# A two-layer encoder trunk on one core: PSUM evacuation by ACT, a mean ahead of a weight split, and a later retention turn

## Chip, cores and metric

The kernel runs on one core of a Trainium2 chip. The metric is the device time of one execution in microseconds (us); smaller is better.

## The reference, cut to what matters

Two layers work on x of 256 positions by 1024 features. Each layer is a half-step SwiGLU FFN, a mixer, and another half-step FFN; every part begins with an RMSNorm whose scale, shift and gate come from a conditioning vector c.

```python
for l in range(DEPTH):                                        # DEPTH = 2
    cond = (silu(c) @ ada_w[l] + ada_b[l])                     # 9 vectors of 1024
    sh1, sc1, g1, sh2, sc2, g2, sh3, sc3, g3 = jnp.split(cond, 9)
    x = x + 0.5 * g1 * swiglu(modulate(rmsnorm(x, norm_g[l, 0]), sh1, sc1), ffn1_w13[l], ffn1_w2[l])
    x = x + g2 * hybrid_mixer(modulate(rmsnorm(x, norm_g[l, 1]), sh2, sc2), w_in[l], w_out[l], ...)
    x = x + 0.5 * g3 * swiglu(modulate(rmsnorm(x, norm_g[l, 2]), sh3, sc3), ffn2_w13[l], ffn2_w2[l])
return rmsnorm(x, final_g)
```

The mixer projects to four groups (forgetting attention "fox", mLSTM, retention "ret", state space "ssd"), each with four heads of 64, and joins them by w_out. The FFN's inner width is 2816.

## The kernel before

**Layout and precision.** The residual lives transposed in SBUF (xT: eight tiles k of 128 features by 256 positions). Every large product is made of three matmuls per 128-by-128 weight tile (mm3, lines 238 to 240): each operand is a rounded high part and a low remainder, and high x high, high x low and low x high are added. The weights arrive by DMA as raw tiles of 512 KB (four slots, NRAW, issued by SP), and `split` makes the parts: ACT copies raw to whi (line 220), DVE subtracts to wlo (line 221). `wload` is one DMA and one split per raw tile.

**Order.** The program is traced in Python, and a scheduler at compile time lays the instructions out per engine: by priority, which is program order, among those it takes to be ready at that time by its own estimates. On the chip each engine then runs its own list strictly in that order, with semaphores between engines. `tc.add_manual_dep(..., NoSync ...)` adds an edge to that layout alone; it makes no wait of its own. POOL (here: InOrder, line 105 in the profile) keeps the traced order.

**The statistics.** Each RMSNorm is started before its statistics are known: `pre_tile` makes the parts of xT times the scale (uh, ul), and the first projections run on those. In `mm_two` the first pair of projections runs six of the eight tiles k (KS), then `stat_end` puts in the sum of squares (line 367, PE), the mean on ACT (line 388, `stat_rs`), and the power -0.5 on POOL; then the pair goes on with its last two k. The next pair runs KR = 2 tiles k of its first half, and only then `st.rows()` spreads the factors over the partitions by matmuls (line 394) and ACT copies them to R (line 398). PE stands behind POOL's power there. `norm_h` then makes the normed h from R for all later projections. In the FFN the pairs are c = 0, 1, 2; in the mixer they are the projections rq, rk and sx.

**The mixer's steps.** ORDER names the steps one after another: p.x is the projection of x, the others work on its results. Steps with a `yield` are continued each time their name comes again. PSUM has four banks of tag a (projections), three of tag b (everything small in the mixer and R) and one of tag c (sums). `row_sums` turns the gate sums into rows: a bank b, two copies by ACT (lines 860 and 861) and one subtraction by DVE from PSUM (line 862), of eight partitions. `ret_front` then wants three banks b (lines 1131 and 1136). `put_y` is the way of each mixer's result y to the output projection: four transposes into a bank b (`to_fm`, line 817), a copy to yh by ACT (line 827) and a subtraction to yl by DVE from PSUM (line 828). Retention's result ry is made at step rg (line 1247) and turned there at once. The tag "cin" of the mixer's pool has one slot; `copied` uses it to take the convolutions' inputs out of PSUM (line 1147).

**Background loads.** The conditioning vectors of later parts are made beside the main work: `ada_load` is a DMA of 512 KB (araw) and a reduction on DVE (line 279). BG holds how many such loads follow each projection: pairs (m, n) mean n loads over the next m calls of `background`. In the mixer one araw slot is used (MB = 1).

Of the kernel before, what the change touches and what calls it, by code (L numbers as in the profile page):

```python
# [9 lines left out]
F32 = mybir.dt.float32  # L10
F32R = mybir.dt.float32r
AF = mybir.ActivationFunctionType
# [35 lines left out]
NRAW = 4  # L48
NSP = 3
KS = 6  # L50
KR = 2
BG = [((16, 17), (1, 0), (7, 14), (3, 4)), ((8, 0), (6, 13)), ((2, 0), (13, 18), (5, 0), (10, 14)), ((2, 0), (13, 18), (5, 0), (10, 14)),
      ((8, 0), (6, 8)), ((3, 0), (14, 8))]
R0 = 6
MB = 1
NW = 11, 0, 2, 6
# [1 line left out]
LF = 10  # L58

ORDER = """p.rq p.rk h clear p.sx p.mv rqe rke rq gates rk p.sbc mv sxe sx sbc p.rv rv p.mq rows ssd ret p.mk ssd mq ret  # L60
 p.sz ssd mk mlstm p.rg sz ssdb p.fk rg mlstm p.fq ssdb fk mlstm p.fv fq mlstm fox p.mo fv fox mo""".split()

WO_STEPS = {1: "fox", 3: "turn", 5: "turn"}
RAW = ("rq", "rk", "sx")
# [5 lines left out]
def trunk_kernel(  # L70
# [134 lines left out]


    spare = [None, 0]

    def split(raw):

        a, b = raw.shape[1:]
        v = lambda t: t[:, : a * b].rearrange("p (a b) -> p a b", a=a)
        pl, n = wp, NHW
        if spare[0] is not None:
            spare[1] = (spare[1] + 1) % (NHW + NSP)
            if spare[1] >= NHW:
                pl, n = spare[0], NSP
        hi = v(pl.tile([P, HW], F32R, tag="whi", name="whi", bufs=n))
        lo = v(pl.tile([P, HW], F32R, tag="wlo", name="wlo", bufs=n))
        act.activation(out=hi, in_=raw, func=AF.Copy)  # L220
        dve.tensor_tensor(out=lo, in0=raw, in1=hi.bitcast(F32), op=ALU.subtract)  # L221
        return hi, lo

    def raw_tile():
        return wp.tile([P, HW], F32, tag="raw", name="raw", bufs=NRAW)

    def wload(src, n, a, b):

        out = []
        for i in range(n):  # L230
            raw = raw_tile()[:, : a * b]
            sp.dma_start(out=raw, in_=src[:, i * a * b:(i + 1) * a * b])
            out.append(split(raw.rearrange("p (a b) -> p a b", a=a)))
        return out

    def mm3(o, w, x, first, last, **kw):
# [149 lines left out]
    def stat_rs(sums):  # L386
        v = tp.tile([P, 2], F32, tag="rs", name="rs")
        act.activation(out=v, in_=sums, func=AF.Identity, scale=1.0 / D, bias=epsc)
        pool.tensor_tensor(out=v, in0=v, in1=half[:, :2], op=ALU.pow)
        return v  # L390

# [146 lines left out]
    def ffn_in(fp, l, i, w13, w2, st, done):  # L538
# [20 lines left out]
        if first:  # L559
            h, os = st  # L560
            for c in range(NS):
                o = os[c].rearrange("p (a b) -> p a b", a=2)
                gate_out(c, o[:, 0, :], o[:, 1, :])
        else:
            def evac(c, og, oa):
                v = tp.tile([P, 4], F32, tag="fb", name="fb")
                act.activation(out=v[:, 0:1], in_=oa[:, T:T + 1], func=AF.Copy)
                act.activation(out=v[:, 2:3], in_=og[:, T:T + 1], func=AF.Copy, scale=0.5)
                g = fp.tile([P, T], F32, tag="gR", name="gR", bufs=2)
                a = fp.tile([P, T], F32, tag="aR", name="aR", bufs=2)  # L570
                dve.tensor_tensor(out=g, in0=og[:, :T], in1=st.R, op=ALU.mult)
                dve.tensor_tensor(out=a, in0=oa[:, :T], in1=st.R, op=ALU.mult)
                gate_out(c, a, g, v[:, 0:1], v[:, 2:3])

            pend = None
            for c in range(ND):
                w = wload(w13(l, c), 2, KT, P)
                og, oa = bank_a()[:, :TS], (bank_b() if c < 2 else bank_a())[:, :TS]
                mm_two((og, oa), w, (st.uh, st.ul), st)
                if c:  # L580
                    evac(*pend)
                if c == NN:
                    h = norm_h(st)
                pend = (c, og, oa)
            evac(*pend)
# [146 lines left out]
    def mixers_in(mp, l, st, done):  # L732
# [17 lines left out]

        def proj_first(name):

            w = wload(wfm[l, FM.index(name)], 2, KT, P)
            background()
            os = [bank_a()[:, :TS] for _ in range(2)]
            mm_two(os, w, (st.uh, st.ul), st)
            r = mp.tile([P, 2, TS], F32, tag=dict(rq="rawrq", rk="ml", sx="rl")[name], name="raw" + name)
            for j in range(2):
                act.activation(out=r[:, j, :], in_=os[j], func=AF.Copy)
            return r  # L760
# [63 lines left out]

        def put_y(m, o):
            h = yh[:, m].rearrange("p a b -> p (a b)")
            act.activation(out=h, in_=o, func=AF.Copy)
            dve.tensor_tensor(out=yl[:, m].rearrange("p a b -> p (a b)"), in0=o, in1=h.bitcast(F32), op=ALU.subtract)

        def pv_tm(pt0, pt1, v):  # L830

# [10 lines left out]
        def row_sums(g):  # L842
# [16 lines left out]
            pe.matmul(o[:, T:T + P], lhsT=gi[:, 1, :], rhs=ident, start=False, stop=True)  # L859
            act.activation(out=rows[:8], in_=o[:8, :3 * P], func=AF.Copy)  # L860
            act.activation(out=rt[32:40], in_=o[32:40, :3 * P], func=AF.Copy)
            dve.tensor_tensor(out=rows[32:40], in0=o[32:40, :3 * P], in1=rt[32:40].bitcast(F32), op=ALU.subtract)
            return rows

        def add_row(o, rows, r, first=True, last=False):
# [378 lines left out]
        def e_rg():  # L1244
            r2 = tm_silu2(v["org"], "g2", rw(R_RG, 256))
            y = mp.tile([P, 2, 256], F32, tag="y", name="ry", bufs=2)
            dve.scalar_tensor_tensor(out=y, in0=r2, scalar=0.5, in1=v["rl"].rearrange("p t h d -> p t (h d)"),
                                     op0=ALU.mult, op1=ALU.mult)
            put_y(2, to_fm(y))

        def e_h():
# [176 lines left out]
```

## Time and profile before

| | |
|---|---|
| three runs | 1073.56, 1071.71, 1073.25 us; median 1073.25 us |
| the profiled execution | 1072.46 us, of which the span from the first to the last instruction is 1070.7 us |
| granted TensorE clock | 0.998 of full speed |
| busy: PE / DVE / ACT / POOL | 1049.5 / 857.2 / 544.6 / 65.4 us |

The span is what the profile's rows are measured in; the time around it (1.76 us here) is not in them. Starts in the rows are microseconds from the start of the span. Layer 0's mixer runs from about 208 to 350 us, layer 1's from about 728 to 870 us, so a place in layer 1's mixer lies about 520 us behind its twin. A matmul's listed duration is modelled and overlaps the next one; what counts for PE is the distance from start to start.

### The profile page before, as it was taken

How to read it: one execution, taken by the hardware profiler on the slowest of the kernel's cores; microseconds unless marked ns; L12 is line 12 of the kernel's file. 1: busy time of each engine (PE TensorE's matmuls, PEld its weight loads, DVE VectorE, ACT ScalarE, POOL GpSimd, SP SyncE). 2: the span in 40 equal slices, each digit the busy share in tenths (PEclk: the TensorE clock that was granted, in tenths of full speed). 3: DMA queues.
4: the chain of work that ended last, by engine and by line, in shares of the span. 5: the costliest groups of instructions: out<-in, count | busy, mean ns of one | idle time of the engine just before them, and what ended most of it. 6: DMA issues, size and time to landing. Idle time of an engine off the chain costs nothing. (4 is left out here: it accounts for less than half of the span.)

```text
span 1070.7 us, 21683 instructions
## 1 busy us (share of the span) xinstructions
PE 1049.5 (98%) x8725; PEld 1035.1 (97%) x8725; DVE 857.2 (80%) x1503; ACT 544.6 (51%) x904; POOL 65.4 (6%) x87
## 2 busy tenths in 40 slices
PE   8999999999999999999999999999999999999997
PEld 6999999998999999999999999999999999999997
DVE  6899888699877998888688998767988689866551
ACT  4565544375446745533474543356636466454441
POOL 0000001110101100000100000011000020000010
PEclk9999999999999999999999999999999999999999
DMA  9899888854466689987568998766546366765541
GB/s 365 345 322 358 308 320 301 278 179 148 145 221 211 210 289 328 326 300 274 184 217 288 324 321 295 268 217 190 175 130 217 120 216 231 269 218 186 182 136 40
DMA packets 74023, 258.29 MB, mean 241 GB/s; under 512 B 10178, under 2 KB 12610, under 8 KB 73411
## 3 DMA queue, kind: packets, MB, share of 16 engines
q1 hardware_dynamic: 73634, 256.39, 69.7%
q8 instruction: 68, 1.11, 0.4%
q10 hardware_dynamic: 288, 0.52, 0.1%
q14 instruction: 33, 0.26, 0.1%
HBM read 255.83 MB, written 1.05 MB: 240 GB/s over the span
## 5 line engine op out<-in xcount | busy, mean ns | idle before, releaser
L220 ACT ACTIVATE whi<-raw 128x1024 fp32r<-128x1024 f32 (+1 forms) x340 | 353.5, 1046 | 276.1 <-PE pa L239 69.1
L221 DVE TENSOR_TENSOR wlo<-raw,whi 128x1024 fp32r<-128x1024 f32 (+1 forms) x340 | 409.0, 1209 | 90.3 <-ACT whi L220 89.3
L238 PE MATMUL pa<-hh,whi 128*128 128x256 f32 x1392 | 395.4, 284 | 0.8 <-ACT whi L220 0.8
L240 PE MATMUL pa<-hh,wlo 128*128 128x256 f32 x1392 | 393.1, 282 | 0.5 <-DVE wlo L221 0.5
L239 PE MATMUL pa<-hl,whi 128*128 128x256 f32 x1392 | 392.9, 282 | 0.0
L238 PEld LDWEIGHTS pa<-hh,whi 128*128 128x128 f32 x1392 | 267.0, 192 | 3.2 <-issue 1.8
L240 PEld LDWEIGHTS pa<-hh,wlo 128*128 128x128 f32 x1392 | 265.1, 190 | 0.7 <-DVE wlo L221 0.7
L239 PEld LDWEIGHTS pa<-hl,whi 128*128 128x128 f32 x1392 | 265.0, 190 | 0.6 <-issue 0.5
L279 DVE CUSTOM_DVE_ANT_0 araw<-araw,cact 128x1024 f32<-128x1024 f32 x128 | 156.5, 1224 | 46.8 <-DMA araw<-in_ada_dram 46.5
L238 PE MATMUL pa<-sh,whi 128*128 128x256 f32 x660 | 184.2, 279 | 0.0
L240 PE MATMUL pa<-sh,wlo 128*128 128x256 f32 x660 | 184.2, 279 | 0.0
L239 PE MATMUL pa<-sl,whi 128*128 128x256 f32 x660 | 184.2, 279 | 0.0
L238 PEld LDWEIGHTS pa<-sh,whi 128*128 128x128 f32 x660 | 125.1, 190 | 0.0
L240 PEld LDWEIGHTS pa<-sh,wlo 128*128 128x128 f32 x660 | 125.1, 190 | 0.0
L239 PEld LDWEIGHTS pa<-sl,whi 128*128 128x128 f32 x660 | 125.0, 189 | 0.0
L555 ACT ACTIVATE sh<-s 128x256 fp32r<-128x256 f32 x88 | 36.2, 412 | 102.5 <-DVE s L548 96.7
L105 POOL TENSOR_TENSOR acc<-acc,sq 128x256 f32<-128x256 f32 x40 | 34.5, 862 | 730.1 <-issue 448.8
L784 PE MATMUL pa<-whi,hh 128*128 128x256 f32 (+1 forms) x192 | 55.4, 289 | 0.0
L238 PE MATMUL pa<-uh,whi 128*128 128x258 f32 x192 | 55.2, 288 | 0.0
L786 PE MATMUL pa<-whi,hl 128*128 128x256 f32 (+1 forms) x192 | 54.9, 286 | 0.0
L785 PE MATMUL pa<-wlo,hh 128*128 128x256 f32 (+1 forms) x192 | 54.5, 284 | 0.0
L239 PE MATMUL pa<-ul,whi 128*128 128x258 f32 x192 | 54.3, 283 | 0.0
(295 smaller groups left out, 1439.8 us busy)
## 6 DMA issues: line engine op xcount, KB each, us to landing
araw<-in_ada_dram SPq DMA_DIRECT2D x128, 512.0 KB, 5.5
raw<-in_w13b_dram SPq DMA_DIRECT2D x88, 512.0 KB, 5.2
raw<-in_w13a_dram SPq DMA_DIRECT2D x76, 512.0 KB, 5.7
raw<-in_w2a_dram SPq DMA_DIRECT2D x44, 512.0 KB, 5.8
raw<-in_w2b_dram SPq DMA_DIRECT2D x44, 512.0 KB, 4.7
raw<-in_wfm_dram SPq DMA_DIRECT2D x32, 512.0 KB, 4.8
raw<-in_wtm_dram SPq DMA_DIRECT2D x24, 512.0 KB, 4.6
raw<-in_wo_dram SPq DMA_DIRECT2D x16, 512.0 KB, 4.4
```

What stands on the lines that cost most here:

```text
L105: return lambda **kw: tc.keep_in_program_order(op(**kw))
L220: act.activation(out=hi, in_=raw, func=AF.Copy)
L221: dve.tensor_tensor(out=lo, in0=raw, in1=hi.bitcast(F32), op=ALU.subtract)
L238: pe.matmul(o, lhsT=wh, rhs=xh, start=first, stop=False, **kw)
L239: pe.matmul(o, lhsT=wh, rhs=xl, start=False, stop=False, **kw)
L240: pe.matmul(o, lhsT=wl, rhs=xh, start=False, stop=last, **kw)
L279: dve.tensor_tensor_reduce(out=raw, in0=raw, in1=cact, scale=0.5, scalar=0.0, op0=ALU.mult, op1=ALU.add, accum_out=cond[l][:, i:i + 1])
L555: act.activation(out=sh[:, c, :], in_=s, func=AF.Copy)
L784: pe.matmul(os[t], lhsT=h[0][:, k, ts], rhs=wh[:, y, :], start=(k == 0), stop=False)
L785: pe.matmul(os[t], lhsT=h[0][:, k, ts], rhs=wl[:, y, :], start=False, stop=False)
L786: pe.matmul(os[t], lhsT=h[1][:, k, ts], rhs=wh[:, y, :], start=False, stop=(k == KT - 1))
```

## The change

Five edits:

1. `put_y`: a second ACT copy takes the turned result out of PSUM in full precision (yf, in the slot "cin"), and DVE's subtraction reads yf in SBUF and no longer the bank. This happens four times a layer.
2. `row_sums`: a third ACT copy (rf, also in the slot "cin"), and the subtraction moves from DVE to POOL and reads rf. Once a layer.
3. `stat_rs` remembers its mean instruction; `split` can be laid behind it in ACT's order. This is asked for the second raw tile of the FFN's c = 1 and of the mixer's rk, so that the mean stands in front of that split. KR goes from 2 to 4: twice as many tiles k of the second pair run ahead of `st.rows()`.
4. Retention's step rg ends after ry is made; its turn (`put_y(2, ...)`) follows at a second rg, behind ssd's turn in ORDER.
5. BG of layer 1's mixer: its eight background loads are spread over the last ten projections, where they had been over the last six.

```diff
@@ -48,9 +48,9 @@
 NRAW = 4
 NSP = 3
 KS = 6
-KR = 2
+KR = 4
 BG = [((16, 17), (1, 0), (7, 14), (3, 4)), ((8, 0), (6, 13)), ((2, 0), (13, 18), (5, 0), (10, 14)), ((2, 0), (13, 18), (5, 0), (10, 14)),
-      ((8, 0), (6, 8)), ((3, 0), (14, 8))]
+      ((4, 0), (10, 8)), ((3, 0), (14, 8))]
 R0 = 6
 MB = 1
 NW = 11, 0, 2, 6
@@ -58,7 +58,7 @@
 LF = 10
 
 ORDER = """p.rq p.rk h clear p.sx p.mv rqe rke rq gates rk p.sbc mv sxe sx sbc p.rv rv p.mq rows ssd ret p.mk ssd mq ret
- p.sz ssd mk mlstm p.rg sz ssdb p.fk rg mlstm p.fq ssdb fk mlstm p.fv fq mlstm fox p.mo fv fox mo""".split()
+ p.sz ssd mk mlstm p.rg sz ssdb p.fk rg mlstm p.fq ssdb rg fk mlstm p.fv fq mlstm fox p.mo fv fox mo""".split()
 
 WO_STEPS = {1: "fox", 3: "turn", 5: "turn"}
 RAW = ("rq", "rk", "sx")
@@ -205,8 +205,9 @@
 
 
     spare = [None, 0]
-
-    def split(raw):
+    mean = [None]
+
+    def split(raw, behind=None):
 
         a, b = raw.shape[1:]
         v = lambda t: t[:, : a * b].rearrange("p (a b) -> p a b", a=a)
@@ -218,19 +219,22 @@
         hi = v(pl.tile([P, HW], F32R, tag="whi", name="whi", bufs=n))
         lo = v(pl.tile([P, HW], F32R, tag="wlo", name="wlo", bufs=n))
         act.activation(out=hi, in_=raw, func=AF.Copy)
+        if behind is not None:
+            tc.add_manual_dep(nc.cur_bb.bb.instructions[-1], behind.name, mybir.DependencyInfo(
+                mybir.DependencyClass.NoSync, mybir.DependencyReason.DATA), reason="behind")
         dve.tensor_tensor(out=lo, in0=raw, in1=hi.bitcast(F32), op=ALU.subtract)
         return hi, lo
 
     def raw_tile():
         return wp.tile([P, HW], F32, tag="raw", name="raw", bufs=NRAW)
 
-    def wload(src, n, a, b):
+    def wload(src, n, a, b, behind=None):
 
         out = []
         for i in range(n):
             raw = raw_tile()[:, : a * b]
             sp.dma_start(out=raw, in_=src[:, i * a * b:(i + 1) * a * b])
-            out.append(split(raw.rearrange("p (a b) -> p a b", a=a)))
+            out.append(split(raw.rearrange("p (a b) -> p a b", a=a), behind if i == 1 else None))
         return out
 
     def mm3(o, w, x, first, last, **kw):
@@ -386,6 +390,7 @@
     def stat_rs(sums):
         v = tp.tile([P, 2], F32, tag="rs", name="rs")
         act.activation(out=v, in_=sums, func=AF.Identity, scale=1.0 / D, bias=epsc)
+        mean[0] = nc.cur_bb.bb.instructions[-1]
         pool.tensor_tensor(out=v, in0=v, in1=half[:, :2], op=ALU.pow)
         return v
 
@@ -574,7 +579,7 @@
 
             pend = None
             for c in range(ND):
-                w = wload(w13(l, c), 2, KT, P)
+                w = wload(w13(l, c), 2, KT, P, mean[0] if c == 1 else None)
                 og, oa = bank_a()[:, :TS], (bank_b() if c < 2 else bank_a())[:, :TS]
                 mm_two((og, oa), w, (st.uh, st.ul), st)
                 if c:
@@ -750,7 +755,7 @@
 
         def proj_first(name):
 
-            w = wload(wfm[l, FM.index(name)], 2, KT, P)
+            w = wload(wfm[l, FM.index(name)], 2, KT, P, mean[0] if name == "rk" else None)
             background()
             os = [bank_a()[:, :TS] for _ in range(2)]
             mm_two(os, w, (st.uh, st.ul), st)
@@ -824,8 +829,10 @@
 
         def put_y(m, o):
             h = yh[:, m].rearrange("p a b -> p (a b)")
+            c = mp.tile([P, 2 * T], F32, tag="cin", name="yf")
             act.activation(out=h, in_=o, func=AF.Copy)
-            dve.tensor_tensor(out=yl[:, m].rearrange("p a b -> p (a b)"), in0=o, in1=h.bitcast(F32), op=ALU.subtract)
+            act.activation(out=c, in_=o, func=AF.Copy)
+            dve.tensor_tensor(out=yl[:, m].rearrange("p a b -> p (a b)"), in0=c, in1=h.bitcast(F32), op=ALU.subtract)
 
         def pv_tm(pt0, pt1, v):
 
@@ -859,7 +866,9 @@
             pe.matmul(o[:, T:T + P], lhsT=gi[:, 1, :], rhs=ident, start=False, stop=True)
             act.activation(out=rows[:8], in_=o[:8, :3 * P], func=AF.Copy)
             act.activation(out=rt[32:40], in_=o[32:40, :3 * P], func=AF.Copy)
-            dve.tensor_tensor(out=rows[32:40], in0=o[32:40, :3 * P], in1=rt[32:40].bitcast(F32), op=ALU.subtract)
+            rf = mp.tile([40, 3 * P], F32, tag="cin", name="rf")
+            act.activation(out=rf[32:40], in_=o[32:40, :3 * P], func=AF.Copy)
+            pool.tensor_tensor(out=rows[32:40], in0=rf[32:40], in1=rt[32:40].bitcast(F32), op=ALU.subtract)
             return rows
 
         def add_row(o, rows, r, first=True, last=False):
@@ -1246,6 +1255,7 @@
             y = mp.tile([P, 2, 256], F32, tag="y", name="ry", bufs=2)
             dve.scalar_tensor_tensor(out=y, in0=r2, scalar=0.5, in1=v["rl"].rearrange("p t h d -> p t (h d)"),
                                      op0=ALU.mult, op1=ALU.mult)
+            yield
             put_y(2, to_fm(y))
 
         def e_h():
```

## Rows read from the trace of the kernel before

**Rows 1.** The page: busy us of each engine, share of the span, instructions.
```profile
PE 1049.5 (98%) x8725; PEld 1035.1 (97%) x8725; DVE 857.2 (80%) x1503; ACT 544.6 (51%) x904; POOL 65.4 (6%) x87
```

**Rows 2.** Waits of PE: for whom, us in total, times, longest.
```profile
PE pb L394 <- POOL rs L105: 2.8, 2, 1.5
PE pb L1136 <- DVE rows L862: 2.4, 2, 1.7
PE pb L868 <- DVE fm L1097: 1.5, 1, 1.5
...
PE pb L817 <- DVE ry L1247: 0.8, 1, 0.8
...
PE pb L875 <- DVE yl L828: 0.5, 1, 0.5
```

**Rows 3.** Timeline, layer 1's second FFN starts: start, us, engine, line [idle before].
```profile
873.79 1.99 ACT L220 ACTIVATE whi<-raw 128x1024 fp32r<-128x1024 f32 x2
...
874.82 0.61 PE L367 MATMUL stat<-tab,acc 128*128 128x1 f32 x4
...
876.09 1.06 ACT L220 ACTIVATE whi<-raw 128x1024 fp32r<-128x1024 f32 x1 [0.31 <-DMA raw<-in_w13b_dram]
...
877.06 0.24 ACT L388 ACTIVATE rs<-stat,epsc 128x2 f32<-128x2 f32 x1
...
877.38 1.64 POOL L105 TENSOR_TENSOR rs<-rs,half 128x2 f32<-128x2 f32 x1 [2.61 <-ACT fb L568]
...
879.07 0.71 PE L394 MATMUL pb<-tab,rs 128*128 128x128 f32 x4 [1.36 <-POOL rs L105]
```

**Rows 4.** Timeline of POOL, the same power in layer 1's mixer.
```profile
733.89 0.70 POOL L105 TENSOR_TENSOR rs<-rs,half 128x2 f32<-128x2 f32 x1 [2.13 <-ACT rs L388]
```

**Rows 5.** Timelines of ACT, DVE and PE, the gate rows in layer 0.
```profile
253.47 0.48 ACT L861 ACTIVATE rt<-pb 8x384 fp32r<-8x384 f32 x1
...
256.61 0.55 DVE L862 TENSOR_TENSOR rows<-pb,rt 8x384 fp32r<-8x384 f32 x1
...
257.21 1.16 PE L1136 MATMUL pb<-rq,kz 128*128 128x128 f32 x8 [1.66 <-DVE rows L862]
```

**Rows 6.** Same stretch later: ACT, PE; and busy us (instructions) of PE, PEld, DVE, ACT, POOL.
```profile
265.14 0.60 ACT L989 ACTIVATE pp<-pb 128x512 f32<-128x512 f32 x1
...
265.80 0.49 PE L993 MATMUL pb<-sc,bz 128*128 128x128 f32 x2
...
248.00:268.00 20.00, 18.34 (x134) 17.18 (x134) 19.86 (x46) 11.03 (x17) 0.16 (x1) 1.00 0.46 152
```

**Rows 7.** Timelines of PE and DVE, around ssd's turn in layer 0, and mLSTM's y.
```profile
303.84 0.66 PE L898 MATMUL pb<-tab,pp 128*128 128x128 f32 x4 [0.22 <-ACT pt L895]
...
304.38 0.69 DVE L828 TENSOR_TENSOR yl<-pb,yh 128x512 fp32r<-128x512 f32 x1
...
326.56 0.69 DVE L1240 SCALAR_TENSOR_TENSOR my<-moth,ml 128x512 f32<-128x512 f32 x1
```

**Rows 8.** Timeline of DVE, a background load in layer 1's mixer.
```profile
830.43 1.22 DVE L279 CUSTOM_DVE_ANT_0 araw<-araw,cact 128x1024 f32<-128x1024 f32 x1 [1.55 <-DMA araw<-in_ada_dram]
```

**Rows 9.** Timelines of DVE and PE, the last turn of layer 0 and its reader.
```profile
335.46 1.23 DVE L279 CUSTOM_DVE_ANT_0 araw<-araw,cact 128x1024 f32<-128x1024 f32 x1 [0.67 <-DMA araw<-in_ada_dram]
...
337.36 0.39 PE L239 MATMUL pa<-yl,whi 128*128 128x256 f32 x1 [0.41 <-DVE yl L828]
```

**Rows 10.** Timelines of ACT, DVE and PE, layer 0's mixer starts; and a DMA's landing.
```profile
213.05 0.26 ACT L388 ACTIVATE rs<-stat,epsc 128x2 f32<-128x2 f32 x1 [3.32 <-PE stat L367]
...
215.30 1.22 DVE L279 CUSTOM_DVE_ANT_0 araw<-araw,cact 128x1024 f32<-128x1024 f32 x1 [5.36 <-DMA araw<-in_ada_dram]
...
223.87 1.28 DVE L221 TENSOR_TENSOR wlo<-raw,whi 128x1088 fp32r<-128x1088 f32 x1
...
226.37 0.29 PE L784 MATMUL pa<-whi,hh 128*128 128x272 f32 x1
...
araw<-in_ada_dram SPq DMA_DIRECT2D x1, 512.0 KB, 6.5
```

## The prediction

> **What bounds the kernel now.** I read the page first. PE is busy for 98% of the span, 1049.5 us for 8725 matmuls, so one every 0.12 us [rows 1]; the clock is full throughout. The kernel is bound by PE, and an edit that removes no matmul can only win back time in which PE stands still. That is about 21 us of the span, part of it head and tail. Second comes PE's list of waits: five entries lie where this change works, and they add up to 8.0 us [rows 2]. This is the most that can be had. Third come the timelines around these waits, to see what is late next once one is gone. A gain on PE lasts only if the engine that PE waited for also gets ahead; otherwise PE meets it again at the next semaphore.
>
> **The statistics (edit 3).** In the second FFN of both layers PE waits for POOL's power, 2.8 us in two places [rows 2]. In layer 1 the sums leave PE at 875.4 at the latest (start 874.82 plus 0.61), ACT is free at 875.8, but next in ACT's list is a split whose raw tile has not landed: it runs from 876.09 for 1.06, and the mean comes at 877.06, the power from 877.38 to 879.02, and PE goes on at 879.07 after 1.36 idle [rows 3]. With the mean ahead of that split it runs at about 875.8, the power ends at about 876.1 + 1.64 = 877.7, which is when PE arrives today (879.07 - 1.36). KR = 4 lets two more tiles k, six matmuls or 6 x 0.12 = 0.7 us, run first, so PE arrives at 878.4. The wait is gone with 0.7 to spare: **2.8 us** for both layers. What the code asks for is less: the mean ahead of c = 1's second split, which today runs earlier (by the order of the raw tiles the late split is that of c = 3). If the late one keeps its place, KR alone saves 2 x 0.7 = 1.4. I take 2.8, since holding one split of 1.05 empties ACT's list just ahead of the mean; both stay for the range. The held split itself would end near 877.1 and its subtraction some 1.3 later; PE wants it after a first half of 24 matmuls (2.9) that starts at 877.0 and the spread, near 880.4: hidden. R comes later against PE by 0.7 where there was no wait; DVE's next user of it was behind other work there, so this costs nothing.
>
> The power takes 1.64 there beside DVE's subtractions and 0.70 in the mixer with DVE idle [rows 3, 4]. The Trainium skill (GPSIMD Engine Reference, Specifications) says that GpSimd shares its SBUF interfaces with VectorE and contends with instructions that have two SBUF inputs, which the split's subtraction is; the trace agrees with 1.64 against 0.70. By that rule the moved power stays long, and if the mean does not get ahead of the late split, KR alone cannot cover the wait.
>
> **The gate rows (edit 2).** PE waits 1.66 in layer 0 and 2.4 - 1.7 = 0.7 or 0.8 in layer 1 for the bank that DVE's subtraction frees [rows 2, 5]. ACT had read it at 253.95, DVE came to it only at 256.61, since it works in order through ssd's tables. The third ACT copy (0.48, by its neighbour) frees the bank at about 254.4, so this wait goes. POOL does the subtraction instead: the nearest price is 0.70 to 1.64, and its result is wanted much later by mLSTM, so it is hidden. mq's convolution input shares the slot "cin" and now waits for that, some 2 us; its reader stands behind ret's products in DVE's list, so this is hidden too. What is late next are ssd's exponentials: the second ends at 265.74 and PE's matmul behind its bank starts at 265.80 [rows 6]. They stand in ACT's list behind a tanh that needs DVE, and DVE is busy for 19.86 of 20 us in that stretch [rows 6]. DVE loses only the 0.55 of the moved subtraction [rows 5], so ACT gets ahead by about 0.55 and PE keeps that much: **1.1 us** for both layers, not 2.4. The bounds are these two; the low one is nearer, because the row shows no slack at all at 265.80.
>
> **The later turn and put_y (edits 1 and 4).** PE's wait for ry (0.8, layer 0) and for the bank of ry's turn (0.5, layer 1) go, since the transposes move behind ssd's turn: **1.3 us** [rows 2]. No matmul is added. In the new place two turns and mLSTM's three groups of transposes want banks b one after another. Today the third group waits 0.22 there for ACT [rows 7]. Now ACT has three more copies of 0.6 (the exponential of that shape [rows 6]) in front, and the slot "cin" holds one yf: the second yf must wait for DVE's subtraction of the first, which ends at 305.07 [rows 7], and a bank is then free at 305.7, against a third group that PE would reach at 303.84 + 0.6 = 304.4. Bounds: nothing (the compile-time order puts projection matmuls in between) and 1.2 per layer. I take 0.4, twice today's wait for twice the turns: **0.8 us lost**. At the end of the mixer yl of the last turn comes 0.6 later by its copy. In layer 0 it stood behind a background reduction that ended at 336.69 anyway, and PE waited 0.41 [rows 9]; the copy ends well before, so nothing is added there.
>
> The Trainium skill (VectorE: DVE Perf Modes, Rules for kernel authors) says for elementwise work on matmul output: accept the slower PSUM source, or copy to SBUF first if many operations follow. Here one follows, so the rule speaks against edit 1. The trace bears out that DVE gains nothing: 0.69 from PSUM, 0.69 with both inputs in SBUF [rows 7]. What the copy can bring is the bank's earlier release alone; by the rule the forecast would lose 0.5 and have the new waits at their 2.4, and the sum would be 3.0 instead of 5.1.
>
> **The background loads (edit 5).** In layer 1 PE waits 1.5 for fox's bank [rows 2], behind a DVE that stood 1.55 for a background load's DMA and then reduced it for 1.22 [rows 8]. Of the last four projections' six loads four remain, so this wait probably shrinks: at most 1.5. Against it, two loads of 1.22 more fall into layer 1's twin of the stretch where DVE is full [rows 6]: at most 2.4 lost. With both ends open I take half of the gain: **0.7 us**.
>
> **The sum.** 2.8 + 1.1 + 1.3 - 0.8 + 0.7 = 5.1 us. The profiled execution took 1072.46, so 1067.4; the median is 0.8 above it, so the forecast for the median is **1068.1 us**, 0.5% faster. What this kernel's measurement can tell from no change is about 0.2%, or 2.1 us.
>
> **The rivals.**
>
> B, half: the late split keeps its place ahead of the mean (1.4 instead of 2.8) and the loads bring nothing: 1.4 + 1.1 + 1.3 - 0.8 = 3.0, **1070.2**. For it: the code names another split than the one in the way. Chance 0.18.
>
> C, all: nothing is handed back: 2.8 + 2.4 + 1.3 + 1.5 = 8.0, **1065.2**. For it: the layout is made anew and may put the exponentials ahead. Against it: DVE's 19.86 of 20. Chance 0.09.
>
> D, handed back: PE's gains in the mixers end at a full DVE, with 2.4 for the two background loads and 2.4 at the crowded banks: 2.8 + 1.1 + 1.3 - 2.4 - 2.4 = 0.4, **1072.8**. Chance 0.14.
>
> E, the other side: in the mixer rk's second split now waits for the mean, which ends at 213.3; split and subtraction, 1.06 and 1.28 by their neighbours [rows 3, 10], bring it to 215.6, and only then is its raw slot free for the transfer of mv's second half. If SP keeps that transfer ahead of layer 0's first background load, the load issues after 215.6 and lands 6.5 later, at 222.1 or after, while DVE has its reduction in the list at 215.30 [rows 10]. DVE stands 6.8 us; mv's first subtraction has 226.37 - 225.15 = 1.2 of slack [rows 10], so PE loses 5.6 and the change ends 0.5 above before: **1073.8**. It decides once the load issues more than 5.1 + 1.2 = 6.3 us late. Where B's smaller savings go with it, it is 1073.25 - 3.0 + 5.6 = 1075.9, outside 0.2%; I take that for the likelier form, since the same late split lies behind both. Against it: a load that is ready is normally laid out before one whose slot is not free. Chance 0.11.
>
> **How the numbers follow.** The forecast has 0.48, with a range of its own of 1066.5 (new waits at nothing, the whole 1.5 at fox) to 1069.7 (new waits at 2.4). With B and C it makes the faster side: 0.48 + 0.18 + 0.09 = 0.75. D and 0.04 of E are the same within 0.2%: 0.18; E's likelier form is slower: 0.07. The range that should hold eight times in ten leaves out E, the far side of C and of D: 1064.9 to 1073.1.
>
> **What would show it.** Right: no wait of line 394's matmuls for POOL, the mean within 0.6 us of the end of the sums in both second FFNs, no wait at ret_front's third bank, and a wait of about 1 us at ssd's o0 and o1 banks in its place. ACT has ten more copies, about 5 us in all. DVE stays at 857 less 1.1. Wrong: the mean still behind a split that waits for its DMA (B); DVE idle for a background load at the start of the mixer (E); PE waits at the transposes of mLSTM above 1 us (D). What would break the forecast as a whole is the layout: all engines' lists are made anew, and a misjudged DMA or copy elsewhere can cost PE as much as any one term here.

## The result: 2.5% slower

The median went to 1101.9 us (1093.1 to 1105.5 in four executions) against 1073.4 beside it: a ratio of 1.025, interval 1.022 to 1.028. The forecast was 1068.1, with 1073.1 as the far end of its range. The profiled execution of the changed kernel is the lowest of its four, so what is broken down below is 20.6 of the 28.5 us: its span is 1091.3 against 1070.7.

First the page's busy line, changed kernel:

```profile
PE 1060.2 (97%) x8725; PEld 1042.3 (96%) x8725; DVE 857.0 (79%) x1501; ACT 548.1 (50%) x914; POOL 69.0 (6%) x89
```

PE has as many matmuls as in [rows 1] and is "busy" 10.7 us longer for them, and it stands 10 us longer as well. DVE is busy as long as before and ACT 3.5 us longer. So neither work nor an engine's load explains the loss.

PE's waits, changed kernel (total, times, longest):

```profile
PE pa L244 <- DVE wlo L225: 6.3, 4, 1.9
PE pb L877 <- DVE fm L1106: 4.9, 2, 3.5
PE pa L242 <- DVE xT L447: 3.5, 2, 1.8
PE pa L192 <- DVE warm L186: 1.4, 1, 1.4
PE pb L1001 <- ACT pp L998: 1.3, 1, 1.3
PE pb L844 <- DVE pp L1005: 1.2, 1, 1.2
PE pb L399 <- POOL rs L105: 1.1, 2, 0.8
```

Against [rows 2] the edits did what they say: the gate rows, ry and yl are gone, the power is down from 2.8 to 1.1. Three new lines outweigh them: the low half of a split weight (1.9, some 16 us behind the sums of each of the three later feed-forwards), fm in the mixers, and xT, the residual that frees a bank near a feed-forward's end.

The clock is the other half. The windows of the changed kernel (busy us of PE, PEld, DVE, ACT, POOL with counts; granted clock; DMA share; GB/s) around three of those waits:

```profile
315.00:320.00 5.00, 2.50 (x19) 2.19 (x17) 3.82 (x13) 0.00 (x0) 1.14 (x1) 1.00 0.58 165
320.00:325.00 5.00, 4.04 (x17) 3.69 (x18) 3.67 (x15) 0.00 (x0) 0.50 (x1) 0.66 0.47 161
565.00:570.00 5.00, 3.52 (x27) 3.13 (x25) 4.59 (x12) 4.23 (x10) 0.00 (x0) 1.00 0.12 46
570.00:575.00 5.00, 4.40 (x24) 4.40 (x25) 3.80 (x8) 1.31 (x3) 0.00 (x0) 0.66 0.37 124
905.00:910.00 5.00, 2.74 (x14) 2.14 (x13) 4.75 (x12) 3.19 (x8) 0.00 (x0) 0.84 0.02 7
910.00:915.00 5.00, 5.00 (x37) 5.00 (x37) 3.66 (x7) 3.03 (x7) 0.00 (x0) 0.81 0.61 205
```

A mean of 0.66 over 5 us is 3.4 us at the lower level, 1.2 GHz (0.34 x 5 / 0.5). In the one that begins at 570.5 PE starts a matmul every 0.21 us, and every 0.12 behind it, so by estimate a stretch costs half its length, 1.7. There are four such stretches, two in layer 0's mixer (at about 274 and 321 us) and two in feed-forwards, 6.8 us in all, and each comes while or soon after PE stood. Before, the clock was full up to the last matmul. The other three executions show a mean clock of 0.987 to 0.990 against 0.993 here: more such stretches, worth 3 to 7 of the 7 to 12 us by which they are longer.

Where the time sits is read from the sums of the statistics (PE's four stat matmuls), which cut the program into stages. Lengths in us between their starts, from each run's trace:

| kernel | mixer, layer 0 | second FFN, layer 0 | first FFN, layer 1 | mixer, layer 1 | second FFN, layer 1 |
|---|---|---|---|---|---|
| before | 142.3 | 190.0 | 188.2 | 141.8 | 176.2 |
| changed | 147.6 | 194.0 | 194.3 | 142.2 | 180.1 |
| no hold at all (e1) | 142.5 | 191.0 | 188.7 | 142.1 | 176.1 |
| hold in the FFNs alone (e2) | 142.0 | 200.2 | 192.3 | 142.4 | 177.5 |
| late split held instead (e5) | 142.2 | 190.2 | 188.2 | 144.2 | 174.8 |
| both held (e6) | 142.2 | 196.9 | 197.4 | 142.6 | 182.3 |
| all but the hold in the FFNs (e8) | 147.4 | 190.7 | 188.3 | 142.3 | 175.7 |
| six raw buffers, no hold (e9) | 141.5 | 192.9 | 189.4 | 142.3 | 177.3 |
| six raw buffers, hold (e10) | 143.1 | 189.9 | 188.9 | 142.4 | 176.1 |
| changed, six raw buffers (e13) | 144.9 | 189.6 | 188.3 | 142.9 | 176.2 |
| changed, no hold of rk (e14) | 143.4 | 202.1 | 195.7 | 142.3 | 177.8 |

Three feed-forwards lose 14.0 us and layer 0's mixer 5.3; the start of the program takes 1.1 more, as it does in e11 too, which has no edit there. What the "hold" does is seen in ACT's timeline of the changed kernel at layer 0's second feed-forward, where PE starts the sums at 361.05:

```profile
362.04 1.07 ACT L221 ACTIVATE whi<-raw 128x1024 fp32r<-128x1024 f32 x1 [2.27 <-DMA raw<-in_w13b_dram]
363.01 0.24 ACT L392 ACTIVATE rs<-stat,epsc 128x2 f32<-128x2 f32 x1
363.15 1.05 ACT L221 ACTIVATE whi<-raw 128x1024 fp32r<-128x1024 f32 x1
...
364.15 1.05 ACT L221 ACTIVATE whi<-raw 128x1024 fp32r<-128x1024 f32 x1
...
365.15 1.06 ACT L221 ACTIVATE whi<-raw 128x1024 fp32r<-128x1024 f32 x1
```

The mean still stands behind a split that waits for its DMA, as in [rows 3]: by the order of the raw tiles that is the first split of chunk 3 (c = 3), which was laid out ahead of the mean again. Behind the mean now come three splits, c = 1's second, which the edit holds, and both of c = 2. Their tiles had landed (no wait stands before them); before, all three were split ahead of the mean. And this is SP's list of transfers there, first in the kernel before, then in the changed one (start, time to the last issue of the row, count):

```profile
331.94 20.11 SPq L232 DMA_DIRECT2D raw<-in_w13b_dram  x7
352.14 0.56 SPq L276 DMA_DIRECT2D araw<-in_ada_dram  x1
354.14 7.40 SPq L232 DMA_DIRECT2D raw<-in_w13b_dram  x5
```

```profile
338.08 19.92 SPq L236 DMA_DIRECT2D raw<-in_w13b_dram  x7
358.05 0.90 SPq L280 DMA_DIRECT2D araw<-in_ada_dram  x2
364.40 0.33 SPq L236 DMA_DIRECT2D raw<-in_w13b_dram  x1
365.54 0.33 SPq L280 DMA_DIRECT2D araw<-in_ada_dram  x1
366.68 16.50 SPq L236 DMA_DIRECT2D raw<-in_w13b_dram  x5
```

Both have issued seven weights by then. SP issues in order, and a weight's transfer needs a free raw buffer, of which there are four. With three of them full of tiles that wait for the mean, SP stands from 358.95 to 364.40, 5.5 us, until c = 3's first tile has been subtracted and its buffer is free; before, it went on at 354.14, 1.4 after its last issue. The theory to test, T: the loss of the feed-forwards is that of late transfers, not of the held split itself.

For which tile does PE wait, then? The code puts the second half of c = 1 into a bank b and both halves of c = 2 into banks a. These are rows of PE and DVE in the changed kernel, the two of bank b first:

```profile
366.97 0.29 PE L242 MATMUL pb<-uh,whi 128*128 128x258 f32 x1
...
367.21 0.28 PE L244 MATMUL pb<-uh,wlo 128*128 128x258 f32 x1
...
376.41 1.22 DVE L225 TENSOR_TENSOR wlo<-raw,whi 128x1024 fp32r<-128x1024 f32 x1
...
377.69 0.39 PE L244 MATMUL pa<-uh,wlo 128*128 128x258 f32 x1 [1.95 <-DVE wlo L225]
```

PE takes up the held split (c = 1's second, bank b) without a wait. The wait of 1.95 is for c = 2's second: its high part was made at 365.15 to 366.21 (the last row of ACT above), but its subtraction stands in DVE's list behind the steps that make the normed h (lines 428 and 433) and comes only at 376.41. Its tile had landed long before. So of the feed-forwards' loss the three waits of 1.9 are not waits for a late transfer; T can hold for the waits for xT.

### The profile page after: what moved, and what is told of

The parts are those of the page before. It is cut to its first block, busy times and chain, and to the rows that moved or that the text cites. A ratio compares the mean times of both kernels' runs of the same rounds, so it can differ in the third digit from the quotient of the medians.

```text
span 1091.3 us, 21671 instructions
## 1 busy us (share of the span) xinstructions
PE 1060.2 (97%) x8725; PEld 1042.3 (96%) x8725; DVE 857.0 (79%) x1501; ACT 548.1 (50%) x914; POOL 69.0 (6%) x89
## 4 chain that ended last, share of the span: by engine, by line
PE 72%; DVE 11%; issue 7%; DMA 6%; ACT 2%; POOL 1%; SPq 0%; DVEq 0%; POOLq 0%; ACTq 0%
PE pa L244 21%; PE pa L242 21%; PE pa L243 21%; DVE wlo L225 4%; DMA araw<-in_ada_dram 3%; DMA raw<-in_w13b_dram 2%; PE pa L791 1%; PE pa L789 1%; PE pa L790 1%; ACT whi L221 1%; DMA raw<-in_w13a_dram 1%; DVE cva L722 1%; DVE ul L421 1%; PE pb L844 1%; DVE araw L283 1%
## 5 line engine op out<-in xcount | busy, mean ns | idle before, releaser
L244 PE MATMUL pa<-uh,wlo 128*128 128x258 f32 x192 | 56.2, 293 | 5.9 <-DVE wlo L225 5.8
```

The costliest lines, as they stand in the source:

```text
L244: pe.matmul(o, lhsT=wl, rhs=xh, start=False, stop=last, **kw)
```

## The experiments

**Which edit (e1 to e4).** The edits of the change, taken out or put in by themselves. Where a run takes or adds a hold, only the call is shown; the part in `split`, `wload` and `stat_rs` goes with it.

e1, the changed kernel without the hold:

```diff
-                w = wload(w13(l, c), 2, KT, P, mean[0] if c == 1 else None)
+                w = wload(w13(l, c), 2, KT, P)
...
-            w = wload(wfm[l, FM.index(name)], 2, KT, P, mean[0] if name == "rk" else None)
+            w = wload(wfm[l, FM.index(name)], 2, KT, P)
```

> The changed kernel without the order mean-before-split at both places; KR = 4 and all other edits stay. Theory T (late loads): the held split frees its raw buffer late, SP's queue stands for 5.5 us behind it, the feed-forward's transfers and splits come late, PE waits 1.9 at the held split and 1.75 at a residual that waits for a late background load, and the clock falls to 0.5 for 3.4 us after such waits. Then the three feed-forward stages between statistics go back to 190, 188 and 176 us, the mixer of layer 0 keeps its 5.2, and the time is 1076 to 1080. Rival R1 (four tiles first): KR = 4 itself makes the layout that comes late; then the time stays at 1093 to 1105. Rival R2 (rk's hold makes the mixer's loss too): 1070 to 1074.

Measured: 1074.2, ratio 1.0032 (1.0017 to 1.0046). The feed-forwards are back, so the hold makes the loss and KR = 4 does not (R1 falls). The mixer is back too, which T had not said; that is R2, though e7 shows below that rk's hold by itself does not make the mixer's loss.

e2, the kernel before with the hold in the feed-forwards alone:

```diff
-                w = wload(w13(l, c), 2, KT, P)
+                w = wload(w13(l, c), 2, KT, P, mean[0] if c == 1 else None)
```

> The kernel before with one edit alone: c = 1's second split behind the mean, in the feed-forwards; KR = 2. T: most of the loss of the three feed-forward stages comes with it, 14 us in a quiet execution and more where the clock falls more often: 1085 to 1098, with PE's waits of about 2 for wlo and a stretch of about 5 us in which SP's queue stands near the statistics. R1: the hold alone does nothing or gains up to 2.8: 1070 to 1074.

Measured: 1090.5, ratio 1.018 (1.015 to 1.021): two thirds of the whole loss from this one line. SP's list and, 140 us later, DVE's near the end of the same feed-forward:

```profile
331.71 20.18 SPq L236 DMA_DIRECT2D raw<-in_w13b_dram  x7
351.99 0.86 SPq L280 DMA_DIRECT2D araw<-in_ada_dram  x2
358.06 0.33 SPq L236 DMA_DIRECT2D raw<-in_w13b_dram  x1
```

```profile
509.11 1.23 DVE L283 CUSTOM_DVE_ANT_0 araw<-araw,cact 128x1024 f32<-128x1024 f32 x1 [2.61 <-DMA araw<-in_ada_dram]
...
513.58 1.22 DVE L283 CUSTOM_DVE_ANT_0 araw<-araw,cact 128x1024 f32<-128x1024 f32 x1 [2.10 <-DMA araw<-in_ada_dram]
...
514.85 0.17 DVE L288 TENSOR_TENSOR cond<-cond,col 128x8 f32<-128x8 f32 x1
...
517.44 0.87 DVE L447 SCALAR_TENSOR_TENSOR xT<-pa,cond,xT 128x256 f32<-128x256 f32 x2
```

SP stands 5.2 us beside the statistics (352.85 to 358.06), PE waits 1.9 at 371.45 for c = 2's second split, as in the changed kernel, and then for over 140 us PE waits for nothing longer than 0.6. But the 32 background loads of this feed-forward lie in the same queue. The second is reduced at 387.9 (before: 381.9), the last at 513.6 (before: 501.6). The residual needs the last one's result; behind it DVE's list has two subtractions (2.4) and then xT, for which PE waits 4.3 at line 242. The clock falls at both waits. The two waits and two falls (an estimated 3.4) make 9.6 of the 10.2 by which this stage grew. That the loads end late because SP stood at the start is likely but not shown: the second load was issued at 352.42, ahead of its time before (361.59), and was reduced late because DVE came to it late, and six of the 12 us arise further on, where the nineteenth load is issued at 456.3 instead of 442.4, behind six weights in SP's list.

e3, put_y, the gate rows and the later turn without the rest; e4, KR = 4 alone:

```diff
-KR = 2
+KR = 4
```

> The kernel before with the edits of the mixer alone: the copies in put_y, the gate rows on ACT and POOL, the later turn; no hold, KR = 2, the background loads as before. T: these make the mixer's loss of 5.2 in layer 0 and 0.4 in layer 1 by themselves (PE's wait of 3.5 for fm, 1.2 for pp, and two stretches of 3.4 us at half the clock): 1077 to 1081. R2: the mixer loses by rk's hold, and without it the edits bring the 1.6 of the prediction or more: 1070 to 1072.

> The kernel before with KR = 4 alone: six matmuls more ahead of the spread of the reciprocal. T: 1071 to 1074; the two waits of line 394 for POOL shrink by 0.7 each. R1: the loss of the feed-forward stages comes with it, 1085 or more.

Measured: e3 1.0021 (1.0006 to 1.0036), e4 1.0031 (1.0015 to 1.0048). Both small, neither the loss and neither a gain; for e3 T's 1077 to 1081 was wrong and so was R2's 1070 to 1072. In e4 the power's waits are gone and this is in their place:

```profile
PE pa L239 <- DVE hl L428: 1.9, 2, 1.0
```

**Which split, and rk (e5 to e8).** e5 holds the split that stood in the way, the first of chunk 3 (`wload` passes the hold to its first tile here):

```diff
-            w = wload(w13(l, c), 2, KT, P)
+            w = wload(w13(l, c), 2, KT, P, mean[0] if c == ND and not first else None)
             o = bank_a().rearrange("p (a b) -> p a b", a=2)
```

> The kernel before with one edit: not c = 1's second split but the first of the chunk behind the double ones (the split that stood in front of the mean and waited for its raw tile) goes behind the mean, in all three feed-forwards; KR = 2, nothing else. PE's order is the one of before. T (what costs is which split is held: c = 1's raw tile had landed, and holding it keeps its raw buffer and those of c = 2 from SP; the late tile frees nothing late): the mean runs within 0.7 us of the sums, PE's waits for POOL of 1.4 in both second feed-forwards go, and the time is 1.5 to 2.8 below before. Rival R3 (any split held behind the mean costs, since the layout takes it as a wait of ACT): 5 us or more above before.

Measured: 1.0001 (0.9986 to 1.0015). R3 falls: a split held behind the mean costs nothing if its tile is not there anyway. But T's gain did not come either. In layer 0's second feed-forward the mean came 0.9 after the start of the sums (354.9, 355.77) and PE no longer waited for POOL; the stage is 190.2 long as before. PE gave back 0.7 at the first matmuls on hh and hl, whose weight loads now wait for ACT and DVE, and 0.9 for xT, behind a last background load (DVE stood 4.09 for it) that came no earlier. In layer 1's the stage is 1.4 shorter, but in e12, which has no edit there, it is 175.1 as well; and layer 1's mixer is 2.4 longer, with a stretch of 3.4 us at the lower clock. The rows of layer 0:

```profile
371.61 0.19 PEld L242 LDWEIGHTS pa<-hh,whi 128*128 128x128 f32 x1 [0.33 <-ACT hh L432]
372.13 0.19 PEld L243 LDWEIGHTS pa<-hl,whi 128*128 128x128 f32 x1 [0.34 <-DVE hl L433]
```

e6 holds both splits (c = 1's second and that of e5). e7 holds rk's alone, on the kernel before:

```diff
-            w = wload(wfm[l, FM.index(name)], 2, KT, P)
+            w = wload(wfm[l, FM.index(name)], 2, KT, P, mean[0] if name == "rk" else None)
```

e8 is the changed kernel with the first line of e1's edit alone, so without the hold in the feed-forwards:

> The kernel before with both held: c = 1's second split and the late one, so that the mean comes right after the sums and the three splits of landed tiles (c = 1's second, both of c = 2) follow it by 1.4 us earlier than in the run that held c = 1's alone. T: SP's stand beside the statistics shrinks from 5.2 by about 1.4, and the loss with it: 4 to 14 us above before. Rival R4 (the loss came from the mean standing still behind the late split): back to 1070 to 1074.

> The kernel before with the hold in the mixer alone: rk's second split behind the mean, KR = 2, no other edit. If it makes the mixer's loss: the mixer of layer 0 goes from 142.3 to about 147 between the statistics, a background load lands late in its first 20 us, and the time is 4 to 10 us above before. If it does not (the mixer's loss needs the feed-forward's hold or the mixer's edits as well): 1071 to 1074.

> The changed kernel without the hold in the feed-forwards alone; rk's hold and all other edits stay. T: the feed-forward stages are those of the run without any hold (191, 189, 176) and what is left above it is rk's: 1074 to 1084. Rival (the mixer's loss comes from the feed-forward's hold, by its loads): as the run without any hold, 1073 to 1076.

Measured: e6 1.0195 (1.0174 to 1.0216), 21 us, outside both expectations. The mean came at 355.89 and the three splits 0.7 to 0.8 earlier than in e2, yet SP issued its next weight only at 360.23. A third background load had been laid out ahead of it, and both it and the subtraction that frees the weight's buffer stood behind a reduction on DVE that waited 3.3 for its own load:

```profile
332.27 20.27 SPq L236 DMA_DIRECT2D raw<-in_w13b_dram  x7
352.62 6.79 SPq L280 DMA_DIRECT2D araw<-in_ada_dram  x3
360.23 22.02 SPq L236 DMA_DIRECT2D raw<-in_w13b_dram  x8
```

R4 falls, since the mean did not stand behind a split here; the size that T gave assumed e2's order in SP's list, which the layout had changed. PE's waits are others again: in each feed-forward 2.1 to 2.8 for a bank and 2.8 to 3.1 for the low half of c = 3's first split, whose high part was done 14 us before and whose subtraction had gone behind the normed h's steps. They make 16.8, and the clock is low for 24 us. e7: 1.0025 (1.0014 to 1.0036), layer 0's mixer 143.9. e8: 1.0054 (1.0035 to 1.0073), layer 0's mixer 147.4: rk's hold and the other edits together make the mixer's loss, each alone does not. DVE's list in e8 shows it at the mixer's end:

```profile
313.91 1.23 DVE L283 CUSTOM_DVE_ANT_0 araw<-araw,cact 128x1024 f32<-128x1024 f32 x1 [3.84 <-DMA araw<-in_ada_dram]
```

The products for fm wait behind this reduction in DVE's order, and PE waits 3.4 for fm. In e1 the same reduction runs at 310.58. The last of the four products also stands behind a step (hv) for which DVE waits 1.55 for POOL, here and in the changed kernel; in e1 it is ahead of that step, and PE waits 0.9.

**The raw buffers (e9 to e11, e13).** e9 and e10 have six raw buffers in the feed-forwards, in the room of one pair of split buffers, without and with the hold:

```diff
-NSP = 3
+NSP = 2
...
     def raw_tile():
+        if spare[0] is not None:
+            turn[0] = (turn[0] + 1) % (NRAW + 2)
+            if turn[0] >= NRAW:
+                return spare[0].tile([P, HW], F32, tag="raw", name="raw", bufs=2)
```

> The kernel before, no hold; in the feed-forwards two more raw buffers (six instead of four) in the room of one pair of split buffers (six pairs instead of seven). The control for the next run. T: SP runs further ahead, and little else changes: 1066 to 1078.

> The same six raw buffers, and c = 1's second split held behind the mean as in the changed kernel's feed-forwards. T (the hold costs by the raw buffers that it keeps from SP): with two buffers more SP's queue no longer stands 5 us there, and the hold costs less than 5 us against the run with six raw buffers, instead of 19. Rival R5 (the hold costs by PE's own wait for the held split and by the clock that falls after it, whatever SP does): again 15 us or more.

Measured: e9 1.0061 (1.0038 to 1.0084), e10 1.0016 (1.0004 to 1.0028). The same line that cost 1.8% with four raw buffers costs nothing with six; the kernel is 0.45% faster with it, since in e9's layout the mean stands behind a late split and PE waits 5.6 for the power. SP's list in e10, PE's first wait, and ACT around the mean:

```profile
333.20 22.63 SPq L242 DMA_DIRECT2D raw<-in_w13b_dram  x10
355.87 0.62 SPq L286 DMA_DIRECT2D araw<-in_ada_dram  x1
361.10 2.60 SPq L242 DMA_DIRECT2D raw<-in_w13b_dram  x3
```

```profile
PE pa L250 <- DVE wlo L225: 3.6, 4, 1.4
```

```profile
356.76 0.26 ACT L398 ACTIVATE rs<-stat,epsc 128x2 f32<-128x2 f32 x1 [1.57 <-PE stat L377]
358.75 1.06 ACT L221 ACTIVATE whi<-raw 128x1024 fp32r<-128x1024 f32 x1 [1.73 <-DMA raw<-in_w13b_dram]
```

SP still stands, 4.6 us, but ten weights of this feed-forward were issued before, where e2 had seven. PE's wait for c = 2's second split is gone, 1.3 is left in this stage for one of c = 3, and the stage is 189.9 long: R5's 15 us are not there. But the runs do not show T pure either, because more buffers change the order too. By the addresses in the program SP now fetches c = 2's second, both tiles of c = 3 and c = 4's first ahead of c = 1's second. So c = 2's second is split ahead of the mean, and the held split is the one in the last row, which waits 1.73 for its own tile; e9's late split is the same one. Holding a tile that is late costs nothing, as in e5. What six buffers show is that the loss is not in the hold as such. Whether with four it is the kept buffers, or the order of DVE's and SP's lists that comes with them, is not separated.

e11 holds another landed split, c = 2's second, on the kernel before; PE's order stays that of before:

```diff
-                w = wload(w13(l, c), 2, KT, P)
+                w = wload(w13(l, c), 2, KT, P, mean[0] if c == 2 else None)
```

> The kernel before with another split held: c = 2's second behind the mean. PE's order is that of before, and one landed raw tile is held instead of three. T: its buffer is free 2 us later, SP stands about 2 instead of 5.2 near the statistics, and the loss is 0 to 5 us. R5: PE wants this split 6 us later than c = 1's, so no wait of PE and no loss: 1070 to 1074.

Measured: 1.0016 (1.0004 to 1.0028). Within both expectations, so it tells nothing apart; one landed tile costs at most 3 us here.

e13, the changed kernel with six raw buffers:

> The changed kernel, with six raw buffers in the feed-forwards instead of four, in the room of one pair of split buffers. T: the hold there no longer costs, and what is left is the mixers' loss with rk's hold: 1074 to 1084, as the changed kernel without the hold in the feed-forwards (1077.5). Rival R5: 1093 or more.

It has e9's edit on top of the whole change. Measured: 1077.7, ratio 1.0066 (1.0044 to 1.0087): 5.9 us above before instead of 28.5, so 22.6 are back with every edit still in. The three feed-forwards are as long as before; layer 0's mixer is 144.9, so some 2.7 of the 22.6 are its. SP's order is e10's, so what was said there holds here too.

**The rest (e12, e14 to e16).** e12 is the gate rows alone:

```diff
-            dve.tensor_tensor(out=rows[32:40], in0=o[32:40, :3 * P], in1=rt[32:40].bitcast(F32), op=ALU.subtract)
+            rf = mp.tile([40, 3 * P], F32, tag="cin", name="rf")
+            act.activation(out=rf[32:40], in_=o[32:40, :3 * P], func=AF.Copy)
+            pool.tensor_tensor(out=rows[32:40], in0=rf[32:40], in1=rt[32:40].bitcast(F32), op=ALU.subtract)
```

e14 is the changed kernel with the second line of e1's edit alone, so without rk's hold. e15 is e5's edit and the later turn (the ORDER and the yield of the change) on the kernel before, e16 e7's edit and e12's.

> The kernel before with the gate rows alone (third copy on ACT, subtraction on POOL). The prediction's step: PE's wait of 2.4 at line 1136 goes and 1.1 of it is kept: 1070.5 to 1071.5. Rival R6 (the mixers end at DVE's chain of background loads and at fm, which start no earlier): the waits go and the mixers' lengths between statistics, 142.3 and 141.8, stay: 1072 to 1074.

> The changed kernel without rk's hold alone. If rk's hold makes the mixer's 5 us together with the mixer's edits: that mixer comes back to 142.5 from 147.5, and the time is 1094 to 1099. If the feed-forward's hold makes it as well: unchanged at 1100 to 1103.

> The kernel before with the late split held behind the mean and the later turn: PE's waits for the power (2.8) and for ry and its bank (1.3) go, and no landed split is held. By the sum of the waits 1068; if the background loads' chain sets the ends of the stages, as the run with the late split held alone suggests, 1071 to 1074.

> The kernel before with rk's hold and the gate rows, no hold in the feed-forwards, no other edit. If these two make the loss of layer 0's mixer: its length goes from 142.3 to about 147 and the time is 4 to 7 above before. If the copies in put_y or the later turn are needed: 1073 to 1076.

Measured: e12 1.0028 (1.0013 to 1.0044). The wait at line 1136 is gone, and the mixers are 144.7 and 142.8 long instead of 142.3 and 141.8; the forecast's kept 1.1 is not there, but R6, which had the lengths unchanged, is not right either. In layer 0 PE now has these (view of its waits from 212 to 358 us):

```profile
PE pb L870 <- DVE fm L1099: 1.8, 1, 1.8
PE pb L817 <- DVE ry L1249: 1.3, 1, 1.3
PE pb L994 <- ACT pp L991: 1.1, 1, 1.1
```

e14: 1092.0 (1087.7 to 1099.6), ratio 1.019 (1.013 to 1.025); layer 0's mixer is back at 143.4. The time is a little below what was expected, with a spread too wide to split the difference. In its profiled execution layer 0's second feed-forward is 202.1, 8 longer than in the changed kernel, with a wait of 4.9 for xT: the same hold costs the three feed-forwards 14 us in one layout, 16 in e2's and 21 in this one. e15: 1.0002 (0.9989 to 1.0016), though the waits for the power, ry and yl's bank are gone; the sum of the waits, 1068, was not reached. e16: 1.0028 (1.0013 to 1.0044) with 143.2 for the mixer, so the gate rows are not the partner of rk's hold; the copies in put_y, the later turn, KR = 4 and the background loads are left, and which of them it is stays open. No version tried beats the kernel before.

## Why the prediction was wrong

**The step that failed** is the price of the hold: "The held split itself would end near 877.1 and its subtraction some 1.3 later; PE wants it ... near 880.4: hidden". For that one split it was right: PE takes it up without a wait (366.97 above). But it was taken as the whole price, and what the hold does to everything behind it had no term. Both splits of c = 2 went behind the mean too. The three kept three of the four raw buffers, so SP's next weight came 3.4 us after the start of the sums, where before it came 0.6 ahead of it; and c = 2's second was subtracted only behind the normed h's steps. In the profiled execution that shows as 5.8 us of waits for this split, 3.5 for xT and two stretches at the lower clock (an estimated 3.4), and 14.0 in the lengths of the feed-forwards. The hold costs 18 us put in by itself (e2), and 23 come back when it is taken out of the changed kernel (e8). How much of that is the buffers' and how much the new order's stays open. Rival E had one mechanism, a raw slot freed late, but only in the mixer and for one slot; its place and price were wrong: rk's hold alone (e7) costs 0.25%, and the first background load of layer 0's mixer, which E had late, is reduced 0.6 us after the start of the sums in the changed kernel and 2.8 after before.

**The statistics, 2.8.** Rival B's doubt was right: the late split kept its place. The wait fell by 1.7, and by KR = 4 rather than the hold (2.4 is left of it in e2). "R comes later against PE by 0.7 ... costs nothing" failed: e4 shows 1.9 for hl in its place. And where the mean did get ahead (e5), nothing was gained in the time; in layer 0 the stage ends at the chain of background loads, which came no earlier.

**The gate rows, 1.1.** The wait went, and about 1 us came back at ssd's banks, as was said (1.1 in e12, 1.3 in the changed kernel); but others came with it further down, and alone the edit makes the kernel 0.28% slower (e12).

**The later turn, 1.3, and put_y, -0.8.** ry and yl are gone from the list; e15 shows that this shortens nothing that can be measured. Rival D's mechanism, waits handed on, fits what e12 and e15 show of the mixer's edits.

**The background loads, 0.7,** were not run by themselves. Layer 1's mixer changed by 0.4 in all, and the wait that was to shrink, PE's for fm there, is 1.47 where it was 1.49.

**"The clock is full throughout"** was read as a property of the kernel. In the changed kernel it fell in four stretches, at or soon after waits of PE that the kernel before did not have, and by the estimate above 6.8 of the 20.6 us are that.

**"DVE at 857 less 1.1, ACT about 5 more"**: 857.0 and 548.1 (before 544.6); of the copies only 3.5 shows, and DVE lost 0.3.

## What to carry to other kernels

When a step is held back, its own reader is the least of it. Ask which steps go behind it too, which buffers they all keep, and which in-order lists stand behind those buffers (here SP's transfers and DVE's subtractions); then read the new order of every engine before trusting the edit, since one added edge lays out all of them anew. A wait that is taken from the busiest engine is a gain only if the stage's end moves: read what the stage ends on (here a chain of small loads, each issued only when the reduction of an earlier one has freed its slot) before adding up waits. In a kernel at 98% a new wait can be paid twice, since the clock can fall with it.

## What the runs showed of the hardware

PE's longest wait inside the kernel before was 1.66, and its clock did not fall before the last matmul. In the changed kernel the waits of 3.46 (to 320.96), 1.94 (to 570.60) and 1.94 (to 908.68) came with a fall, and so did one of 1.16 (to 271.08); those of 1.95 (to 377.69) and 1.76 (to 520.26) did not. In e9 a wait of 2.77 (to 359.48) came with a fall and one of 2.84 (to 884.13) did not. So the length of one wait alone does not decide it.

The power on two columns has no fixed price. It took 1.64 in [rows 3], 1.60 in the changed kernel and 0.74 in e5, each time among DVE's subtractions, and 0.70 with DVE idle [rows 4]. In both cases below it ends 0.56 after the end of the subtraction that was running when it started. Where that one had just begun, the power is long; where it was about to end, the power is short, though the next subtraction follows at once:

```profile
363.14 1.23 DVE L225 TENSOR_TENSOR wlo<-raw,whi 128x1024 fp32r<-128x1024 f32 x1 [3.16 <-ACT whi L221]
...
363.33 1.60 POOL L105 TENSOR_TENSOR rs<-rs,half 128x2 f32<-128x2 f32 x1 [2.34 <-ACT rs L392]
```

```profile
355.06 2.35 DVE L225 TENSOR_TENSOR wlo<-raw,whi 128x1024 fp32r<-128x1024 f32 x2
...
356.09 0.74 POOL L105 TENSOR_TENSOR rs<-rs,half 128x2 f32<-128x2 f32 x1 [1.24 <-ACT rs L392]
```

The first pair is the changed kernel (363.14 + 1.23 = 364.37; the power ends at 364.93), the second e5, whose first subtraction ends at about 356.27 (the power ends at 356.83). The Trainium skill (GPSIMD Engine Reference, Specifications) says that the two engines contend for SBUF where an instruction of VectorE has two SBUF inputs; the runs agree, and in these two the wait is for the instruction in progress, not for those that follow. The prediction's sentence that the moved power stays long does not follow from it.
